# Hybrid attention / SSD / mixture-of-experts block: 1 / rms out of the SSD rows, one routing step less, combine and loads moved

## The chip, the cores and the metric

One core of a Trainium2 chip. The time is device microseconds of one execution of the whole program.

## The reference

One layer over 256 tokens of width 1024, in float32:

```
h = rmsnorm(x);  proj = h @ w_in      # q k v, indexer, z, xBC, dt, two gates
A: top-64 keys per query by an indexer under a block-causal mask, attention over them
B: conv, SiLU, chunked SSD scan, + D * x,
   yf = y * silu(z);  y_ssd = yf * rsqrt(mean(yf^2 per group of 512) + eps) * g   # 4 groups
merged = sigmoid(g_a) * (y_attn @ w_a) + sigmoid(g_b) * (y_ssd @ w_ssd)
x = x + merged @ w_out
h2 = rmsnorm(x);  top-1 of 4 expert groups, top-2 of its 8 experts, SwiGLU (hidden 256)
x = x + sum over the chosen experts of weight * down(silu(gate) * up)
```

The 2048 columns of y_ssd are four groups; each row (token) has one rsqrt per group.

## The kernel before, in words

All products up to W_out are made in three passes of split operands: each float is a high part plus a low part, and `PASSES` (L233) multiplies high-high, high-low, low-high. Weights of the projections come as chunks (class `Chunk`, L130): `raw` tiles are loaded on SP's queue (tag R, 4 buffers), ScalarE copies the high part (L152), VectorE or GpSimd (POOL) subtracts the low part (L156), into split tiles (tag S, 6 buffers). `next_w` (L219) also starts the load and the split of the chunk after the one that it hands out, so on SP's queue the weights of a chunk stand one chunk ahead of its products. A scheduler orders each engine's instructions by priorities and a timeline of its own; `tc.issue_after(i)` holds the block behind instruction i on i's engine.

The stages: attention with its projections; the SSD branch; the branch products; W_out with the residual and the router's logits; routing; the experts.

*SSD branch.* For each group g, four projection chunks (`xs_chunk`, `z_chunk`) are interleaved with `steps`: x (transposes), e (decays), y and T. `ssd_y` (L738) makes 512 columns in a tile yg: py products of 64 rows, L755 and L756 on VectorE, then the square (L758, ScalarE) into the z tile, whose tag has two buffers, and the sum over columns (L760 to L763, POOL). `ssd_tail` (L765) sums over partitions (ps_n), takes the power -0.5 on POOL, spreads r over all partitions by two products with the identity (ps_r, L775), multiplies yg by gain and r (L781, VectorE), and splits it into yT (L783 on ScalarE, L784 on VectorE).

*Branch products* (L826 to L847). yT holds 16 blocks of 128 columns. Loops: half of the SSD columns i (outside), half of the output columns c, halves of the tokens t. `wide_chunk` (L283) accumulates 8 blocks in one PSUM bank per t, token half 1 lagging by 3 blocks. L832 multiplies by the gate (tanh + 1); for i = 0 POOL adds it to the attention part (L834), for i = 1 VectorE does (L836), TensorE transposes and the result is split into mT.

*Loads of expert weights.* There are 8 quarters of 4 experts, 12 tiles each (8 gate/up, 4 down) of 1 MB, 96 in all, loaded by `prefetch` (L255) on SP's queue behind the last raw load traced so far. `PF0`, `PF1` and `PFO` (L1189 to L1199) say at which step how many tiles go into which buffers: tag E into space of their own, X into the space that the SSD pools leave (`xp`, L823), L into yT's buffers, then H, A, R, S, G. After the first 25 tiles all buffers are given out, and each later tile takes the buffer of a used one (`ring`, L1013).

*Routing and experts.* `route` (L935) finds for each token half the group (L942 to L946), the two experts and the slots; Dm is the 0/1 matrix of tokens by slots. `gather` (L1026) makes the normalised rows of the slots, x1 times Dm, VectorE moves them to xg (L1033); `gate_up` (L1035) multiplies. In quarter 0 `GA` (L1172) gives the order of gathers and gate/ups, and `combine` (L985: 11 VectorE and 3 ScalarE instructions and a transpose) is held behind `routed`, the last Dm. One float32 product shows as two records on TensorE.

Of the kernel before, what the change touches and what calls it, by code (L numbers as in the profile page):

```python
# [11 lines left out]
F32 = mybir.dt.float32  # L12
# [4 lines left out]
ALU = mybir.AluOpType  # L17
# [31 lines left out]
def block_kernel(ctx, tc, xin, idn, ngain, catt, cprep, cssd, cmoe, cwr, wsm, wwide, win, wgu, wdn, out, dbg=None):  # L49
# [633 lines left out]
    snorm = C("snorm")  # L683
    yT = [bigt([P, 2, 4, T], F32R, f"yT{g}") for g in range(4)]
# [53 lines left out]
    def ssd_y(g, q):  # L738
# [3 lines left out]
        st_[g, q, "yg"] = yg  # L742
# [3 lines left out]
        for h2 in range(2):  # L746
# [9 lines left out]
            dve.tensor_tensor(yg[:, h2, :], yg[:, h2, :], zs[:, h2, :], op=ALU.mult)  # L756
        sq = zs_t[g, q]
# [7 lines left out]
    def ssd_tail(g):  # L765
# [4 lines left out]
        r = ssd.tile([P, 2], F32, tag="nv", name="nv")  # L770
        dve.tensor_scalar(r, ps_n, 1.0 / 512, 4 * EPS, op0=ALU.mult, op1=ALU.add)
        power(r, r, None)
        ps_r = paux.tile([P, T], F32, tag="n", bufs=1, name="ps_r")
        for t in range(2):
            pe.matmul(ps_r[:, t * P:(t + 1) * P], lhsT=r[:, t:t + 1].to_broadcast([P, P]), rhs=ident,  # L775
                      start=True, stop=True)
        for q in range(2):
            yg = st_[g, q, "yg"]
            for b in range(2):
                ct = 4 * g + 2 * q + b  # L780
                dve.scalar_tensor_tensor(yg[:, b, :], yg[:, b, :], snorm[:, ct:ct + 1], ps_r, op0=ALU.mult, op1=ALU.mult)  # L781
            hl = yT[g][:, :, 2 * q:2 * q + 2]
            act.copy(hl[:, 0], yg)  # L783
            dve.tensor_sub(hl[:, 1], yg, hl[:, 0].bitcast(F32))  # L784
# [41 lines left out]
    for i in range(2):  # L826
        for c in range(2):
            ps = wide_chunk("S", yT[2 * i:2 * i + 2], LAG)
            for t in range(2):
                ta, tb = tab[t, c][:, 0], tab[t, c][:, 1]  # L830
                m = mo2.tile([P, 512], F32, tag="y", name="mg")
                dve.scalar_tensor_tensor(m, tb, 1.0, ps[t], op0=ALU.add, op1=ALU.mult)  # L832
                if i == 0:
                    pool.tensor_add(ta, m, ta)  # L834
                    continue
                dve.tensor_add(m, m, ta)  # L836
# [9 lines left out]
            if i:  # L846
                prefetch(PF1[2 * c] + PF1[2 * c + 1])  # L847

# [86 lines left out]
    def route(t):  # L935
# [9 lines left out]
        dve.tensor_scalar(gv[:, t, :], gv[:, t, :], gf[:, t:t + 1], -1e30, op0=ALU.is_lt, op1=ALU.mult)  # L945
# [68 lines left out]
    for q in range(8):  # L1014
# [26 lines left out]
        if q:  # L1041
            for k in (0, 4):
                gather(k, 4)
        else:
            for k in GA:
                gather(k[0], k[1])
                for kk in range(*k[2:]):
                    gate_up(kk)
# [262 lines left out]
```

## Time and profile before

| | us |
|---|---|
| median of 3 runs | 583.99 |
| the runs | 583.7, 583.99, 587.01 |
| the profiled execution, its own time | 585.1 |
| its span, first to last instruction | 583.3 |
| TensorE busy in it | 552.6 (95%) |
| VectorE / ScalarE / POOL busy | 330.9 / 271.8 / 239.5 |
| mean granted clock of TensorE | 0.987 |

The page gives one execution: busy time per engine, the span in slices, DMA queues, the chain of work that ended last, and the costliest groups of instructions. Times inside it count from the span's start. A busy TensorE is not TensorE at its peak, since matmuls overlap and their ends are modelled.

### The profile page before, as it was taken

The page shows a single profiled execution, that of the slowest core. Times are in us where ns is not written, and L with a number is a line of the kernel's source. Part 1 is how long each engine was busy: PE and PEld are TensorE (multiplying, and loading weights), DVE is VectorE, ACT ScalarE, POOL GpSimd, SP SyncE. Part 2 cuts the span into 40 slices and gives each one's busy share as a digit, 9 for nine tenths or more (in the row PEclk, how much of TensorE's full clock was granted, in tenths as well). Part 3 has the DMA queues.
Part 4 walks back from the last instruction along what each step waited for, and adds up shares of the span by engine and source line. Part 5 has one row for each costly group of instructions (what it writes and reads, how often), then busy time and mean ns, then how long its engine had stood idle before and what let it go on. Part 6 is the DMA issues. An engine that isn't in the chain of part 4 may idle for free.

```text
span 583.3 us, 9898 instructions
## 1 busy us (share of the span) xinstructions
PE 552.6 (95%) x3605; PEld 400.6 (69%) x3605; DVE 330.9 (57%) x689; ACT 271.8 (47%) x633; POOL 239.5 (41%) x254
## 2 busy tenths in 40 slices
PE   8999989999999999999999999999998898988976
PEld 5878768798898999898878888964453452433512
DVE  3659975999996778989695657451111121111101
ACT  7567557757987877878764436410000000000001
POOL 4687584775844456656567745210000000000000
PEclk9999999999999999999999999999989997999989
DMA  7755244453435488645568589989999999999993
GB/s 272 250 162 169 103 147 146 144 174 124 128 122 186 149 323 334 217 149 185 208 194 300 177 307 389 405 344 417 419 417 408 420 417 421 409 415 421 420 407 123
DMA packets 35123, 159.27 MB, mean 273 GB/s; under 512 B 4096, under 2 KB 5760, under 8 KB 25856
## 3 DMA queue, kind: packets, MB, share of 16 engines
q1 hardware_dynamic: 33776, 157.30, 71.8%
q10 hardware_dynamic: 1296, 1.30, 0.7%
q8 instruction: 30, 0.49, 0.3%
q14 instruction: 21, 0.17, 0.1%
HBM read 157.54 MB, written 1.05 MB: 272 GB/s over the span
## 4 chain that ended last, share of the span: by engine, by line
PE 69%; DMA 12%; DVE 9%; issue 4%; POOL 3%; ACT 3%; SPq 0%; ACTq 0%; POOLq 0%; DVEq 0%
PE ps_S L294 8%; PE pgu L1037 6%; PE ps_xs L241 6%; PE ps_g L294 6%; DMA we<-wdn 5%; DMA we<-wgu 5%; PE ps_z L241 5%; PE py L1097 4%; PE ps_A L294 4%; PE acc L1112 4%; PE ps_g L1030 4%; PE ps_q L294 3%; PE ps_o L241 2%; PE ps_o L294 2%; PE ps_iq L294 2%
## 5 line engine op out<-in xcount | busy, mean ns | idle before, releaser
L156 POOL TENSOR_TENSOR w_hl<-w_raw,w_hl 128x512 fp32r<-128x512 f32 (+1 forms) x101 | 141.6, 1406 | 81.8 <-ACT w_hl L152 66.5
L152 ACT CAST w_hl<-w_raw 128x512 fp32r<-128x512 f32 (+1 forms) x212 | 125.7, 620 | 46.4 <-PE ps_S L294 18.5
L156 DVE TENSOR_TENSOR w_hl<-w_raw,w_hl 128x512 fp32r<-128x512 f32 (+1 forms) x111 | 100.4, 911 | 38.7 <-ACT w_hl L152 38.1
L1055 POOL TENSOR_TENSOR dc<-Dm,cmr 128x128 f32<-128x128 f32 x16 | 6.1, 401 | 143.5 <-DVE Dm L960 137.4
L1037 PE MATMUL pgu<-we,xg 128*32 128x512 f32 x512 | 60.2, 603 | 3.9 <-DMA we<-wgu 3.9
L241 PE MATMUL ps_z<-hT,w_hl 128*128 128x256 f32 x384 | 51.7, 286 | 0.0
L241 PE MATMUL ps_xs<-hT,w_hl 128*128 128x256 f32 x384 | 50.7, 285 | 0.0
L241 PEld LDWEIGHTS ps_z<-hT,w_hl 128*128 128x128 f32 x384 | 47.8, 190 | 2.0 <-issue 2.0
L241 PEld LDWEIGHTS ps_xs<-hT,w_hl 128*128 128x128 f32 x384 | 47.6, 191 | 2.1 <-issue 2.1
L294 PE MATMUL ps_g<-w_hl,gT 128*128 128x512 f32 x192 | 48.1, 399 | 0.0
L294 PE MATMUL ps_S<-w_hl,yT 128*128 128x512 f32 x192 | 44.6, 391 | 0.0
L1033 DVE TENSOR_TENSOR xg<-ps_g,cmoe 128x512 f32<-128x512 f32 (+2 forms) x18 | 11.3, 631 | 57.4 <-PE ps_g L1030 57.4
L1030 PEld LDWEIGHTS ps_g<-Dm,x_sb 128*128 128x128 f32 x256 | 31.0, 191 | 14.9 <-issue 9.7
L294 PEld LDWEIGHTS ps_g<-w_hl,gT 128*128 128x128 f32 x192 | 34.9, 188 | 9.3 <-DVE w_hl L156 1.0
L294 PEld LDWEIGHTS ps_S<-w_hl,yT 128*128 128x128 f32 x192 | 35.8, 188 | 7.4
L1037 PEld LDWEIGHTS pgu<-we,xg 128*32 128x32 f32 x512 | 15.1, 110 | 37.1 <-issue 26.1
L1097 PE MATMUL py<-we,aTt 128*32 128x512 f32 (+1 forms) x272 | 35.8, 616 | 3.8 <-DVE aTt L1083 2.1
L1108 ACT COPY y<-py 128x512 f32<-128x512 f32 (+1 forms) x9 | 4.8, 539 | 66.9 <-PE py L1097 66.9
L1075 DVE SCALAR_TENSOR_TENSOR ac<-th,pgu 128x256 f32<-128x256 f32 x8 | 3.4, 421 | 57.5 <-ACT th L1073 57.5
L1112 PE MATMUL acc<-y,dcT 128*128 128x512 f32 (+1 forms) x68 | 32.6, 606 | 0.9 <-DVE y L1110 0.8
L1030 PE MATMUL ps_g<-Dm,x_sb 128*128 128x128 f32 x256 | 33.4, 280 | 0.0
L1073 ACT ACTIVATE th<-pgu,rs 128x256 f32<-128x256 f32 x8 | 3.8, 474 | 55.1 <-PE pgu L1037 55.1
(296 smaller groups left out, 968.9 us busy)
## 6 DMA issues: line engine op xcount, KB each, us to landing
we<-wgu SPq DMA_DIRECT2D x55, 1024.0 KB, 13.8
w_raw<-wwide SPq DMA_DIRECT2D x60, 512.0 KB, 3.9
w_raw<-win SPq DMA_DIRECT2D x44, 512.0 KB, 3.9
we<-wdn SPq DMA_DIRECT2D x17, 1024.0 KB, 17.4
we<-wdn SPq DMA_DIRECT2D x28, 512.0 KB, 12.0
we<-wgu SPq DMA_DIRECT2D x18, 512.0 KB, 10.2
x_sb<-xin SPq DMA_DIRECT2D x2, 512.0 KB, 4.4
we<-wdn SPq DMA_DIRECT2D x4, 256.0 KB, 11.5
```

What stands on the lines that cost most here:

```text
L152: return act.copy(self.hl[i][:, 0], self.raw[i])
L156: return eng.tensor_sub(hl[:, 1], self.raw[i], hl[:, 0].bitcast(F32))
L241: pe.matmul(ps, lhsT=lhs[k][:, a], rhs=rhs[k][:, b], start=j == 0 and k == 0 and i == 0, stop=j == len(regions) - 1 and k == KD - 1 and i ...
L294: pe.matmul(ps[t], lhsT=lhs[t][k][:, a], rhs=w[k][:, b], start=k == 0 and i == 0, stop=k == KD - 1 and i == 2)
L1030: pe.matmul(ps[:, kk, :], lhsT=x1[:, t, (k + kk) * P:(k + kk + 1) * P], rhs=Dm[:, t].rearrange("p e j -> p (e j)"), start=t == 0, stop=t == 1)
L1033: dve.tensor_tensor(xg[:, ks, :], ps, fgain[:, ks].unsqueeze(2).to_broadcast([P, n, P]), op=ALU.mult)
L1037: i = pe.matmul(pgu[32 * e:32 * e + 32, :], lhsT=xg[:, k, 32 * e:32 * e + 32], rhs=wg[k][e], start=k == 0, stop=k == KD - 1, tile_position ...
L1055: pool.tensor_tensor(dc[:, t], Dm[:, t], cmr[:, t, 4 * q:4 * q + 4].unsqueeze(2).to_broadcast([P, 4, NSLOT]), op=ALU.mult)
L1073: act.activation(th, pgu[:, 0:256], AF.Tanh, scale=rs)
L1097: i_py = pe.matmul(py[32 * e:32 * e + 32, :], lhsT=aTt[:, f, 32 * e:32 * e + 32], rhs=wd[2 * n + f][e][:, c], start=f == 0, stop=f == 1, t ...
L1108: act.copy(y, py)
L1112: pe.matmul(acc[t][n][:, c], lhsT=dcT[:, t * P:(t + 1) * P], rhs=y, start=False, stop=q == 7 and c.stop == 512)
```

## The change

`ssd_y` splits yg times gain into yT at once; `ssd_tail` keeps only r, in a small tile rg. The branch products run with the column half c outside and accumulate each group of 4 blocks in a bank of its own; what comes out of PSUM is multiplied there by r of its group. The tiles of gate b get "+ 1" once. The host's order of the weights follows. One X tile is loaded behind each of the first three chunks, two L tiles behind the fourth and two behind W_out's first. In `route`, the table `gio` is scaled by 1e30 and one instruction takes the place of two. In quarter 0 the gathers of k = 0 and 1 and the first gate/up come first, `combine` is held behind the second eviction, and the gathers of k = 2, 3 and 4 to 7 behind the gate/up before them.

```diff
@@ ssd_y
+        hl = yT[g][:, :, 2 * q:2 * q + 2]
+        for b in range(2):
+            ct = 4 * g + 2 * q + b
+            act.activation(hl[:, 0, b], yg[:, b], AF.Copy, scale=snorm[:, ct:ct + 1])
+            dve.scalar_tensor_tensor(hl[:, 1, b], yg[:, b], snorm[:, ct:ct + 1], hl[:, 0, b].bitcast(F32),
+                                     op0=ALU.mult, op1=ALU.subtract)
         sq = zs_t[g, q]
@@ ssd_tail
-        r = ssd.tile([P, 2], F32, tag="nv", name="nv")
+        r = rg[:, g]
         dve.tensor_scalar(r, ps_n, 1.0 / 512, 4 * EPS, op0=ALU.mult, op1=ALU.add)
         power(r, r, None)
-        ps_r = paux.tile([P, T], F32, tag="n", bufs=1, name="ps_r")
-        for t in range(2):
-            pe.matmul(ps_r[:, t * P:(t + 1) * P], lhsT=r[:, t:t + 1].to_broadcast([P, P]), rhs=ident,
-                      start=True, stop=True)
-        for q in range(2):
-            yg = st_[g, q, "yg"]
-            for b in range(2):
-                ct = 4 * g + 2 * q + b
-                dve.scalar_tensor_tensor(yg[:, b, :], yg[:, b, :], snorm[:, ct:ct + 1], ps_r, op0=ALU.mult, op1=ALU.mult)
-            hl = yT[g][:, :, 2 * q:2 * q + 2]
-            act.copy(hl[:, 0], yg)
-            dve.tensor_sub(hl[:, 1], yg, hl[:, 0].bitcast(F32))
@@ branch products
-    for i in range(2):
-        for c in range(2):
-            ps = wide_chunk("S", yT[2 * i:2 * i + 2], LAG)
-            for t in range(2):
+    for c in range(2):
+        for t in range(2):
+            act.activation(tab[t, c][:, 1], tab[t, c][:, 1], AF.Copy, bias=1.0)
+        U = [mo2.tile([P, 512], F32, tag="y", name="mg") for _ in range(2)]
+        for i in range(2):
+            w = pairs(next_w(), slice(0, 512))
+            src = pairs(yT[2 * i:2 * i + 2], slice(0, T))
+            pss = {}
+            for k in range(KD + LAG):
+                for t in range(2):
+                    kk = k - LAG * t
+                    if not 0 <= kk < KD:
+                        continue
+                    g = kk // 4
+                    if kk % 4 == 0:
+                        pss[t, g] = (pacc.tile([P, 512], F32, tag=f"acc{t}1", name="ps_S") if g
+                                     else pmm.tile([P, 512], F32, tag="mm", name="ps_S"))
+                    for a, b in PASSES:
+                        pe.matmul(pss[t, g], lhsT=src[kk][:, a, t * P:(t + 1) * P], rhs=w[kk][:, b],
+                                  start=kk % 4 == 0 and (a, b) == PASSES[0], stop=kk % 4 == 3 and (a, b) == PASSES[2])
+            for g, t in ((0, 0), (0, 1), (1, 0), (1, 1)):
                 ta, tb = tab[t, c][:, 0], tab[t, c][:, 1]
-                m = mo2.tile([P, 512], F32, tag="y", name="mg")
-                dve.scalar_tensor_tensor(m, tb, 1.0, ps[t], op0=ALU.add, op1=ALU.mult)
-                if i == 0:
-                    pool.tensor_add(ta, m, ta)
+                ps, m, r1 = pss[t, g], U[t], rg[:, 2 * i + g, t:t + 1]
+                if 2 * i + g == 0:
+                    act.activation(m, ps, AF.Copy, scale=r1)
+                elif 2 * i + g < 3:
+                    dve.scalar_tensor_tensor(m, ps, r1, m, op0=ALU.mult, op1=ALU.add)
+                    if i:
+                        dve.tensor_mul(m, m, tb)
+                        pool.tensor_add(ta, m, ta)
+                if 2 * i + g < 3:
                     continue
+                dve.scalar_tensor_tensor(m, ps, r1, tb, op0=ALU.mult, op1=ALU.mult)
                 dve.tensor_add(m, m, ta)
...
-            if i:
-                prefetch(PF1[2 * c] + PF1[2 * c + 1])
+            prefetch(PF1[2 * c + i])
@@ route
-        dve.tensor_scalar(gv[:, t, :], gv[:, t, :], gf[:, t:t + 1], -1e30, op0=ALU.is_lt, op1=ALU.mult)
-        dve.tensor_tensor(em[:, t].rearrange("p (g e) -> p g e", g=4), E[:, t].rearrange("p (g e) -> p g e", g=4),
-                          gv[:, t].unsqueeze(2).to_broadcast([P, 4, 8]), op=ALU.add)
+        dve.scalar_tensor_tensor(em[:, t].rearrange("p (g e) -> p g e", g=4),
+                                 gv[:, t].unsqueeze(2).to_broadcast([P, 4, 8]), gf[:, t:t + 1],
+                                 E[:, t].rearrange("p (g e) -> p g e", g=4), op0=ALU.subtract, op1=ALU.add)
@@ experts, quarter 0
-            for k in GA:
-                gather(k[0], k[1])
-                for kk in range(*k[2:]):
-                    gate_up(kk)
+            gathered = [gather(0, 1), gather(1, 1)]
+            i_gu = gate_up(0)
+            for k, n, a, b in GA:
+                with tc.issue_after(i_gu.ins):
+                    gather(k, n)
+                for kk in range(a, b):
+                    i_gu = gate_up(kk)
         if q == 0:
-            with tc.issue_after(routed.ins):
+            with tc.issue_after(gathered[1].ins):
                 combine()
@@ tables
-GA = ((0, 1, 0, 0), (1, 1, 0, 1), (2, 2, 1, 2), (4, 4, 2, 4))
+GA = ((2, 2, 1, 2), (4, 4, 2, 4))
-PF1 = ("X", "X", "X", "L")
-PFO = ("L", "L", "L", "")
+PF1 = ("X", "X", "X", "LL")
+PFO = ("LL", "", "", "")
```

## Rows read from the trace of the kernel before

**Rows 1.** The page's line of memory traffic, 40 slices of 14.6 us.
```profile
GB/s 272 250 162 169 103 147 146 144 174 124 128 122 186 149 323 334 217 149 185 208 194 300 177 307 389 405 344 417 419 417 408 420 417 421 409 415 421 420 407 123
```

**Rows 2.** The chain that ended last, 480 to 583: start us, us, what.
```profile
541.82 19.88 DMA we<-wgu
...
561.74 1.94 PE pgu L1037 x8
```

**Rows 3.** Stretches: engines' busy us (count), granted clock, DMA share, GB/s.
```profile
340.00:388.00 48.00, 47.74 (x298) 40.74 (x297) 27.69 (x77) 20.52 (x52) 16.11 (x15) 1.00 1.00 390
388.00:391.00 3.00, 3.00 (x27) 1.87 (x30) 0.75 (x3) 0.00 (x0) 0.76 (x2) 1.00 0.51 128
391.00:392.00 1.00, 1.00 (x9) 0.21 (x2) 0.00 (x0) 0.00 (x0) 0.00 (x0) 1.00 0.69 287
392.00:561.70 169.70, 151.56 (x1067) 67.17 (x1066) 28.07 (x66) 10.40 (x22) 5.31 (x14) 0.97 1.01 417
```

**Rows 4.** SP's queue, timeline 380 to 390: start us, us, what.
```profile
380.67 0.42 SPq L270 DMA_DIRECT2D we<-wgu  x1
...
389.39 0.33 SPq L270 DMA_DIRECT2D we<-wgu  x1
```

**Rows 5.** The same table by stretches: branch products, late SSD stage.
```profile
307.40:352.80 45.40, 45.40 (x208) 37.76 (x209) 26.60 (x39) 20.50 (x36) 28.04 (x24) 1.00 0.78 262
216.00:280.00 64.00, 63.84 (x523) 58.47 (x522) 60.73 (x105) 50.28 (x113) 40.73 (x35) 1.00 0.65 229
```

**Rows 6.** The chain that ended last, 186 to 320: a tail's broadcast products.
```profile
292.88 0.64 PE ps_r L775 x4
```

**Rows 7.** Timeline of TensorE, 261 to 262: another tail's broadcast products.
```profile
261.59 0.61 PE L775 MATMUL ps_r<-ident,nv 128*128 128x128 f32 x4
...
262.04 0.27 PE L716 MATMUL ps_x<-ident,xs 128*128 128x128 f32 x1
```

**Rows 8.** VectorE by form, 200 to 360: busy us, mean ns, idle before.
```profile
L784 DVE TENSOR_TENSOR yT<-yg,yT 128x512 fp32r<-128x512 f32 x8 | 7.8, 974 | 0.3 <-ACT yT L783 0.3
...
L606 DVE SCALAR_TENSOR_TENSOR xs<-xs,acc 128x256 f32<-128x256 f32 x10 | 7.0, 716 | 0.0
...
L781 DVE SCALAR_TENSOR_TENSOR yg<-yg,cssd,ps_r 128x256 f32<-128x256 f32 x16 | 6.6, 473 | 0.1
...
L832 DVE SCALAR_TENSOR_TENSOR mg<-tab,ps_S 128x512 f32<-128x512 f32 x8 | 5.3, 678 | 1.7 <-PE ps_S L294 1.7
```

**Rows 9.** ScalarE by form, 200 to 360.
```profile
L783 ACT CAST yT<-yg 128x512 fp32r<-128x512 f32 x8 | 5.1, 637 | 0.9 <-DVE yg L781 0.9
...
L701 ACT ACTIVATE zs<-ps_z 128x256 f32<-128x256 f32 x12 | 4.7, 390 | 7.2 <-DVE zs L702 4.7 <-POOL ysum L761 1.7 <-POOL ysum L763 0.6
```

**Rows 10.** ScalarE by form, 0 to 140.
```profile
L501 ACT ACTIVATE tab<-ps_g,rh 128x512 f32<-128x512 f32 x8 | 5.4, 686 | 0.5 <-PE ps_g L294 0.5
...
L184 ACT ACTIVATE gT<-ps_h,gcol 128x256 fp32r<-128x256 f32 x8 | 3.1, 484 | 0.0
```

**Rows 11.** Timelines 381 to 404: routing steps, first gather, first gate/up.
```profile
383.62 0.35 DVE L945 TENSOR_SCALAR gv<-gv,gf 128x4 f32<-128x4 f32 x2
383.88 0.32 DVE L946 TENSOR_TENSOR em<-logit,gv 128x32 f32<-128x32 f32 x2
384.11 0.31 DVE L948 MAX8 rm<-em 128x8 f32<-128x32 f32 x2
...
386.38 1.95 PE L1030 MATMUL ps_g<-Dm,x_sb 128*128 128x128 f32 x16
...
387.25 0.29 DVE L1033 TENSOR_TENSOR xg<-ps_g,cmoe 128x128 f32<-128x128 f32 x1
...
388.26 1.07 PE L1037 MATMUL pgu<-we,xg 128*32 128x512 f32 x8
```

**Rows 12.** SP's queue, timeline 316 to 338: weights and the first X loads.
```profile
316.28 2.15 SPq L141 DMA_DIRECT2D w_raw<-wwide  x2
...
337.84 1.24 SPq L270 DMA_DIRECT2D we<-wdn  x1
```

More of the change, by code (lines that the diff above doesn't have):

```diff
@@ L683, in block_kernel @@
     snorm = C("snorm")
+    rg = cst.tile([P, 4, 2], F32, name="rg")
     yT = [bigt([P, 2, 4, T], F32R, f"yT{g}") for g in range(4)]
@@ L741, in ssd_y @@
         yg = ssd.tile([P, 2, T], F32, tag="yg", name=f"yg{g}{q}", bufs=YB)
-        st_[g, q, "yg"] = yg
         if q == 0:
@@ L1032, in gather @@
             ks = slice(k, k + n)
-            dve.tensor_tensor(xg[:, ks, :], ps, fgain[:, ks].unsqueeze(2).to_broadcast([P, n, P]), op=ALU.mult)
+            return dve.tensor_tensor(xg[:, ks, :], ps, fgain[:, ks].unsqueeze(2).to_broadcast([P, n, P]), op=ALU.mult)
         def gate_up(k):
@@ L1252, in prep @@
     halves = [slice(0, 512), slice(512, 1024)]
-    wide += [wa[:, :, o] for o in halves] + [ws[:, 8 * i:8 * i + 8, o] for i in range(2) for o in halves]
+    wide += [wa[:, :, o] for o in halves] + [ws[:, 8 * i:8 * i + 8, o] for o in halves for i in range(2)]
     wwide = np.stack(wide + [wo[:, :, 0:512]])
@@ L1274, in prep @@
         "cos": c16, "sin": s16,
-        "gio": _bcast(np.arange(4, 0, -1).astype(f)),
+        "gio": _bcast(np.arange(4, 0, -1).astype(f) * f(1e30)),
         "sio": _bcast(np.where(np.arange(1, 33) <= CAP, np.arange(1, 33), -1).astype(f)),
```

## The prediction

> **What bounds the kernel now.** Three views, in this order. The first is the page's line of memory traffic over forty slices of 14.6 us: about 100 to 330 GB/s in the first half, then over 400 from slice 27 to the last but one [rows 1]. So the last 190 us could be a stage that waits for expert weights. The second, the chain that ended last, says so: it ends in long pieces of expert transfers, the last of them landing at 561.74 us, and only then comes TensorE's tail of 21.6 us to the end of the span [rows 2]. The third, a table by stretches, says when this stream begins and whether it ever stops [rows 3]: the DMA engines are full from 340 to 388 us (share 1.00), half idle from 388 to 391 (128 GB/s), and full again from 392 to 561.7 (417 GB/s). The stop is short and decides this case. 25 expert tiles of 1.05 MB fit in the buffers. The last half tile that needed no routed expert was issued at 380.67 us; the next issue on SP is at 389.39 [rows 4], right after the first four gate/up products of expert quarter 0 freed a buffer. From there 71 tiles follow at 1.05 MB / 417 GB/s = 2.51 us each, 178 us, whatever the compute engines do. So the end is the moment at which the first gate/up product is done, plus a fixed stream and a fixed tail. That moment lies at the end of a long stretch in which TensorE is the bound: 63.84 of 64 us busy in the late SSD stage and 45.40 of 45.40 us in the branch products [rows 5].
>
> Two consequences for pricing. TensorE work taken out before 386 us moves the end by its length. Earlier loads alone fill the same 25 buffers sooner and then wait longer, so they are worth little by themselves.
>
> **SSD rows without 1 / rms.** Each of the four tails loses two broadcast products (ps_r, four records each time). Where they cut into the py pairs the chain gives them 0.64 us [rows 6]; where they stand between other products the next one starts 0.45 us after them (261.59 to 262.04) [rows 7]. Two tails are of each kind: 2 x 0.64 + 2 x 0.45 = **2.2 us** of TensorE removed. The bounds are 4 x 0.45 = 1.8 and 4 x 0.64 = 2.6; I take 2.1, a little under the middle, because some of the 0.64 is the py pair's own restart.
>
> VectorE loses sixteen L781 (473 ns, one input in PSUM) and eight L784 (974 ns): 7.6 + 7.8 = 15.4 us. It gains sixteen 128x256 scalar_tensor_tensor whose two tensor inputs both lie in SBUF. The row with that shape is L606: 716 ns mean, against 473 for L781 [rows 8]. So 16 x 0.716 = 11.5 us, and VectorE is relieved by 3.9 us (bounds: relieved by 7.8 us if the new ones cost 473 ns, loaded with 0.2 more if they take the 974 ns of the 512-wide L784). ScalarE loses eight copies of 637 ns (L783 [rows 9]) and gains sixteen scaled copies of 128x256; the scaled copy of that shape into the same type is L184, 484 ns [rows 10]: 7.7 - 5.1 = 2.6 us more, beside TensorE. Both engines lie beside TensorE here (60.73 and 50.28 us busy of 64 [rows 5]), so I count neither; what it costs if that cover goes is the slower rival below, what it brings if VectorE was the hidden bound the faster one.
>
> In the branch products each of the four (token half, column half) pairs now needs four evacuations instead of two. VectorE gains, per pair, one scalar_tensor_tensor from PSUM (678 ns, L832) and one product of two SBUF tiles (974 ns by L784, the same operands) [rows 8]: 4 x 1.65 = 6.6 us. ScalarE gains a scaled copy out of PSUM (686 ns by L501 [rows 10]) and one "plus 1" of the same size: 4 x 1.37 = 5.5 us. VectorE has 45.4 - 26.6 = 18.8 us free there and ScalarE 24.9 [rows 5], so this is hidden, price 0; the price if a quarter of the 12.1 us came through is +3. The wait that is added is ScalarE's, on a half-done chunk; behind it in its queue stand weight casts, which TensorE needs. The early half of a chunk is read while the late half still accumulates in another bank, so no PSUM buffer is held longer than before. The order of chunks (column half outside) makes the first half of mT early and leaves the last chain, two VectorE operations and four transposes, as it was: 0.
>
> **One routing step less.** In each of two interleaved chains a tensor_scalar goes (383.62 to 383.88, 0.26 us for the pair), and a tensor_tensor becomes a scalar_tensor_tensor (its pair takes 0.23 us, 383.88 to 384.11) [rows 11]. L945 is a whole step of the chain: -0.26, and I give back 0.03 for the longer instruction: **-0.23 us** (bounds 0 and -0.3).
>
> **Combine behind the first gather.** TensorE's sixteen gather records start at 386.38, so the first four, k = 0, are out by 386.38 + 4 x 0.122 = 386.87; its eviction starts only at 387.25, between combine's VectorE instructions, and TensorE runs all sixteen before the first gate/up at 388.26 [rows 11]. After the change only eight records precede it: TensorE is free at 387.36, the eviction (0.29 us) can run from about 387.05, and the gate/up starts near 387.45: **-0.8 us** (bounds 0, if the eviction stays at 387.25 and the order holds, and -1.0, TensorE's eight records). Combine moves 11 VectorE and 3 ScalarE instructions some 1.2 us later. The evictions k = 2 to 7 queue behind it on VectorE, POOL's dc and TensorE's transposes of it behind them; between its first use and now lie the gate/ups of k = 0 to 3, 4 x 1.07 = 4.3 us, so 0.
>
> **Loads from the first chunk on.** SP takes its queue in order. The X loads move from 337.84 us, behind the fourth chunk's weights, to behind the second chunk's (316.28) and the third's [rows 12]. Two of the three are thus done before 340, 2 x 2.51 = 5.0 us less queue, and the 25 tiles are in at about 383.4 instead of 388.4; the last of them cannot come much earlier, because they wait for buffers that W_out's products free up to 380.67. The weights queued behind an X load come up to 2.5 us later. They have a lead of six split tiles, 6 x 1.41 = 8.5 us at 11.3 us (45.4 / 4) per chunk of eight. Price of the move: 0, both ways, except that it makes room for the rest: without it the 3.1 us below could not all be used.
>
> **Sum.** -2.1 - 0.23 - 0.8 = -3.1 us at the first gate/up: its load is issued at 386.3 instead of 389.4, after the buffers are full (383.4), so the stream moves by all of it. The profiled execution took 585.1 us with a span of 583.3; the sum gives 582.0 there. The median of the runs shown is 583.99, 1.1 below, and the forecast goes by it: **580.9 us**. A measurement of this kernel can tell about 1% from no change, 5.8 us; this is half of it.
>
> **Rivals.**
> *The early loads don't come early* (X1 stuck on SP behind SSD buffers still read). The buffers then fill at 388.4 as before, with the next load already waiting: no gap. The gap's worth is what 388 to 392 failed to move, (4 x 417 - 3 x 128 - 287) KB per us = 1.0 MB = 2.4 us: 581.6. Chance 0.1.
> *The loads bound everything*, and the two tiles come straight off the end: 5.0 us, 579.0. Against it the half idle stretch [rows 3]. Chance 0.06.
> *VectorE was the hidden bound of the SSD stage.* The page's chain runs there through VectorE for long pieces, and 60.73 of 64 us is nearly full. Then its 3.9 us come off too: 580.9 - 3.9 = 577.0. Against: TensorE's 63.84 of 64. Chance 0.16.
> *ScalarE late in the SSD stage* (slower). The square of a y step now stands behind two scaled copies, 2 x 0.484 = 0.97 us; POOL's ysum waits for the square, and with two zs buffers the tanh of a later z chunk waits for ysum. L701 already sits idle 7.2 us, of it 1.7 + 0.6 behind ysum [rows 9]. If six z chunks hand on 0.97 us each, 5.8 us, the time is 580.9 + 5.8 = 586.7. It decides once ysum becomes the last to arrive at most z chunks and the delay outlasts the queue of weights. Against: the same steps lose VectorE work. Chance 0.16. A rule stands beside this one: the Trainium skill, "GPSIMD Engine Reference", section 1, says that GpSimd shares its SBUF interfaces with VectorE and contends with VectorE instructions that have two SBUF inputs, as the sixteen new ones have. This trace agrees as far as L606 goes, mean 716 against 473 with a PSUM input; the page gives no price, and by it POOL's adds would be later still.
>
> **How the numbers follow.** The forecast itself has 0.52. Its own range, from the bounds of its terms (-1.8 to -4.0, and 0.5 of run spread), is 579.5 to 582.7. The two outer rivals lie at 577.0 and 586.7; the range 576.5 to 586.5 leaves out some tails of each. Faster by over 1% (under 578.2): most of the VectorE rival and a tail of the forecast, 0.15. Slower by over 1% (over 589.8): the far end of the ScalarE rival, 0.05. The rest is 0.80.
>
> **What would show it.** Right: no ps_r; the first gate/up near 385.2, the expert load behind it near 386.3 and the last landing near 558.6; a longer idle DMA stretch just before that load, ending at the same distance behind it; TensorE still full from 186 to 380. Wrong: TensorE with gaps in the branch products or SSD stage; a first gate/up that moves by much other than 3 us; a last landing that does not move with it.

## The result, and the profile after

The changed kernel takes **587.0 us**, the median of 19 runs (584.95 to 589.77), against 583.92 (582.17 to 587.01, 19 runs) for the kernel before. The ratio is **1.0051**, 95% interval 1.0040 to 1.0062. The forecast was 580.9 us with a range from 576.5 to 586.5: instead of 3.1 us faster it is 3.1 us slower and outside the range. It is half a per cent, within the 1% that the prediction had called no change, but with an interval clear of 1. The profiled execution took 586.69 us, its span is 584.9.

First the stretches of [rows 3] and [rows 5] again (length; busy us and instructions of PE, PEld, DVE, ACT, POOL; granted clock; DMA share; GB/s):

```profile
216.00:280.00 64.00, 63.40 (x513) 57.33 (x512) 62.98 (x101) 50.44 (x116) 40.32 (x36) 1.00 0.65 231
307.40:352.80 45.40, 44.51 (x203) 36.58 (x202) 32.77 (x45) 23.79 (x42) 30.73 (x23) 1.00 0.87 304
392.00:563.00 171.00, 153.54 (x1087) 69.30 (x1079) 28.09 (x67) 10.38 (x22) 5.34 (x15) 0.96 1.01 415
```

TensorE is no longer full: 0.6 us are missing in the late SSD stage, 0.9 in the branch products. VectorE, which was to be relieved of 3.9 us over the SSD stage, has 62.98 us of 64 where it had 60.73. In the branch products it has 32.77 against 26.60, which is near the 6.6 us counted there. What TensorE waited for is in the waits (line and tile, the instruction waited for, us in all, times, longest), the first from 205 to 280, the rest from 300 to 392:

```profile
PE ps_xs L241 <- DVE zs L703: 0.6, 1, 0.6
...
PE ps_o L241 <- ACT w_hl L152: 1.5, 1, 1.5
...
PE ps_lg L929 <- ACT xT L925: 0.9, 2, 0.5
PE ps_n L776 <- POOL ysum L768: 0.9, 1, 0.9
```

These are four places. One product waits for a zs tile near 223 us. The last sum of squares holds up its narrow product at 312 us: the product stands in order among the branch products, so these wait with it. The first narrow product of W_out (its last 512 columns come in two chunks of 256) waits at 359 us. And xT, the transposed rows that the router's product takes, stops TensorE twice at the end of W_out, where before it did once. The timeline of TensorE shows two of them, the wait in brackets:

```profile
313.13 0.61 PE L776 MATMUL ps_n<-ones,ysum 128*128 128x1 f32 x4 [0.90 <-POOL ysum L768]
...
360.74 0.38 PE L241 MATMUL ps_o<-w_hl,mT 128*128 128x256 f32 x1 [1.49 <-ACT w_hl L152]
```

The chain that ended last says why the second is late. The raw weights were issued at 349.82, right behind two of the early L loads (347.48 and 347.95 on SP), landed at 359.97, and ScalarE's cast had been waiting for them:

```profile
349.82 10.15 DMA w_raw<-win
360.03 0.04 issue
360.07 0.63 ACT w_hl L152
```

The next lines are the steps that answer to [rows 11], from timelines of VectorE and TensorE, and the end of the chain, which answers to [rows 2]:

```profile
385.63 0.41 DVE L964 SCALAR_TENSOR_TENSOR em<-gv,gf,logit 128x32 f32<-128x32 f32 x2
385.95 0.31 DVE L967 MAX8 rm<-em 128x8 f32<-128x32 f32 x2
...
388.27 1.05 PE L1049 MATMUL ps_g<-Dm,x_sb 128*128 128x128 f32 x8
389.49 1.07 PE L1056 MATMUL pgu<-we,xg 128*32 128x512 f32 x8 [0.16 <-DVE xg L1052]
```
```profile
545.01 19.85 DMA we<-wgu
564.90 1.11 PE pgu L1056 x8
```

The first gate/up comes at 389.49 instead of 388.26, the load behind it is issued at 390.62 instead of 389.39 [rows 4]. The last load lands at 564.86 (545.01 + 19.85), where 558.6 was forecast.

A table by stage says more than absolute times, because the profiled execution of before had begun its SSD products about 1 us later than every other one here (152.15 us; the others 150.4 to 151.6). All times are from the timelines of TensorE and VectorE (first xs product, first attention product, first W_out product, logit, first gate/up). The last two columns are two kernels of the experiments; they differ in the SSD rework alone.

| us | before | after | e13: order, loads, old tail order | e14: after, old tail order |
|---|---|---|---|---|
| SSD stage (xs to A) | 126.44 | 125.18 | 126.44 | 125.20 |
| attention and branch products (A to W_out) | 74.48 | 76.72 | 74.46 | 76.70 |
| W_out, router (to logit) | 29.51 | 31.82 | 29.04 | 30.29 |
| routing, gather (to gate/up) | 5.68 | 4.91 | 4.90 | 4.90 |
| sum | 236.11 | 238.63 | 234.84 | 237.09 |

The changed kernel gains 1.3 and 0.8 us in the first and last stage and loses 2.2 and 2.3 in the two between: 2.5 us later at the first gate/up, most of the 3.1 us in the medians.

### The profile page after: what moved, and what is told of

Its sections match the earlier page's. It is cut to its first block, busy times and chain, and to the rows that moved or that the text cites. A ratio compares the mean times of both kernels' runs of the same rounds, so it can differ in the third digit from the quotient of the medians.

```text
span 584.9 us, 9882 instructions
## 1 busy us (share of the span) xinstructions
PE 550.2 (94%) x3589; PEld 399.4 (68%) x3589; DVE 341.8 (58%) x687; ACT 277.2 (47%) x649; POOL 245.8 (42%) x254
## 3 DMA queue, kind: packets, MB, share of 16 engines
HBM read 157.54 MB, written 1.05 MB: 271 GB/s over the span
## 4 chain that ended last, share of the span: by engine, by line
PE 56%; DVE 19%; DMA 9%; ACT 6%; issue 5%; POOL 4%; ACTq 0%; SPq 0%; DVEq 0%; POOLq 0%
PE pgu L1056 8%; PE ps_S L840 6%; PE py L1120 5%; DVE w_hl L156 5%; PE ps_g L1049 5%; PE ps_xs L241 4%; PE acc L1135 4%; DMA we<-wdn 3%; DMA we<-wgu 3%; PE ps_z L241 3%; PE ps_o L241 2%; DVE acc L603 2%; PE ps_iq L294 2%; PE ps_A L294 2%; PE ps_k L294 2%
## 5 line engine op out<-in xcount | busy, mean ns | idle before, releaser
L156 POOL TENSOR_TENSOR w_hl<-w_raw,w_hl 128x512 fp32r<-128x512 f32 (+1 forms) x101 | 145.1, 1442 | 77.7 <-ACT w_hl L152 63.4
L156 DVE TENSOR_TENSOR w_hl<-w_raw,w_hl 128x512 fp32r<-128x512 f32 (+1 forms) x111 | 105.4, 958 | 24.2 <-ACT w_hl L152 23.5
L1056 PE MATMUL pgu<-we,xg 128*32 128x512 f32 x512 | 58.5, 595 | 4.9 <-DMA we<-wgu 4.7
L840 PE MATMUL ps_S<-w_hl,yT 128*128 128x512 f32 x192 | 45.1, 392 | 0.0
L1049 PEld LDWEIGHTS ps_g<-Dm,x_sb 128*128 128x128 f32 x256 | 32.5, 197 | 18.0 <-issue 13.6
L1120 PE MATMUL py<-we,aTt 128*32 128x512 f32 (+1 forms) x272 | 38.2, 647 | 4.5 <-DVE aTt L1106 2.6
L1049 PE MATMUL ps_g<-Dm,x_sb 128*128 128x128 f32 x256 | 35.1, 286 | 0.0
L1135 PE MATMUL acc<-y,dcT 128*128 128x512 f32 (+1 forms) x68 | 30.5, 574 | 0.1
```

The lines of the kernel that those rows point to most:

```text
L156: return eng.tensor_sub(hl[:, 1], self.raw[i], hl[:, 0].bitcast(F32))
L840: pe.matmul(pss[t, g], lhsT=src[kk][:, a, t * P:(t + 1) * P], rhs=w[kk][:, b], start=kk % 4 == 0 and (a, b) == PASSES[0], stop=kk % 4 == 3 ...
L1049: pe.matmul(ps[:, kk, :], lhsT=x1[:, t, (k + kk) * P:(k + kk + 1) * P], rhs=Dm[:, t].rearrange("p e j -> p (e j)"), start=t == 0, stop=t == 1)
L1056: i = pe.matmul(pgu[32 * e:32 * e + 32, :], lhsT=xg[:, k, 32 * e:32 * e + 32], rhs=wg[k][e], start=k == 0, stop=k == KD - 1, tile_position ...
L1120: i_py = pe.matmul(py[32 * e:32 * e + 32, :], lhsT=aTt[:, f, 32 * e:32 * e + 32], rhs=wd[2 * n + f][e][:, c], start=f == 0, stop=f == 1, t ...
L1135: pe.matmul(acc[t][n][:, c], lhsT=dcT[:, t * P:(t + 1) * P], rhs=y, start=False, stop=q == 7 and c.stop == 512)
```

## The experiments

Every ratio is to the kernel before on the same chip, with its 95% interval.

**The parts alone.**

`e1`, the changed kernel with the loads in their old places:
```diff
-PF1 = ("X", "X", "X", "LL")
-PFO = ("LL", "", "", "")
+PF1 = ("", "", "XX", "XL")
+PFO = ("L", "L", "L", "")
```


> The changed kernel with the loads of expert weights where they stood before (X, X behind the third branch chunk, X, L behind the fourth, three L along W_out); all else as changed. Theory A (the loads put in front make W_out's narrow weights late: TensorE stops 1.65 us there in the changed kernel, and ScalarE's copies of mT wait behind the cast that waits for them): the 1.65 us stop goes, the first gate/up comes 1.5 to 2 us earlier than 389.5, ratio to the kernel before about 1.002. Theory B (the rebuilt SSD and branch stage costs it, whatever the loads do): the stop stays within 0.5 us, ratio 1.004 to 1.006 as for the whole change.

`e2`, the kernel before with the early loads:
```diff
-            if i:
-                prefetch(PF1[2 * c] + PF1[2 * c + 1])
+            prefetch(PF1[2 * i + c])
...
-PF1 = ("X", "X", "X", "L")
-PFO = ("L", "L", "L", "")
+PF1 = ("X", "X", "X", "LL")
+PFO = ("LL", "", "", "")
```


> The kernel before with the early loads alone. Theory A: TensorE stops before W_out's narrow products as in the changed kernel, the first gate/up comes 1 to 2 us later than 388.3, ratio 1.002 to 1.004. Theory B: no new stop, the buffers fill earlier and wait longer, ratio 0.999 to 1.001.

`e3`, the kernel before with the routing step and the gather order (the hunks of the change at L945 and from L1030 on):
```diff
...
-            for k in GA:
-                gather(k[0], k[1])
...
+            gathered = [gather(0, 1), gather(1, 1)]
+            i_gu = gate_up(0)
...
```


> The kernel before with the routing step less and the new order of the first gathers, gate/ups and combine alone. Both theories: from the first logit step to the first gate/up 0.8 us less than the 5.7 us of before (382.58 to 388.26), the end earlier by about that, ratio 0.9985. A third theory (what moves is what the scheduler places differently anywhere in the program after any edit): TensorE's order changes far from the edit too, and the first logit step moves by more than 0.5 us either way.

`e4`, the changed kernel with those hunks and the loads undone, so that the SSD rework is left:
```diff
...
-            gathered = [gather(0, 1), gather(1, 1)]
...
+PF1 = ("", "", "XX", "XL")
+PFO = ("L", "L", "L", "")
```


> The changed kernel with old routing, old order of the first gathers and old places of the loads: the SSD and branch rework alone. Theory A: 2 us of TensorE gone, less about 1 us that TensorE waits for the last ysum: first gate/up about 1 us earlier than 388.3, ratio 0.998. Theory B: the waits added in the branch stage and in W_out take more than the 2 us: first gate/up 1 us or more later, ratio 1.002 to 1.005.

Measured: e1 1.0077 (1.0050 to 1.0105), e2 1.0029 (1.0006 to 1.0051), e3 **0.9982** (0.9968 to 0.9995), e4 **1.0108** (1.0078 to 1.0137). The order gains what was forecast for it; the SSD rework costs more than the whole change. That the moved loads make the loss falls with e1: without them it is no smaller (the intervals overlap). But e2 is odd, since nothing stops TensorE there before 377 us. Its stretches at the routing stage and its timeline:

```profile
382.00:386.00 4.00, 4.00 (x11) 1.58 (x12) 2.75 (x22) 0.00 (x0) 0.00 (x0) 0.50 1.03 408
```
```profile
378.64 1.16 PE L910 MATMUL ps_lg<-cwr,xT 128*128 128x36 f32 x8 [0.35 <-ACT xT L906]
379.63 0.41 PE L900 MATMUL ps_hf<-ident,x_sb 128*128 128x128 f32 x2
380.50 1.93 PE L910 MATMUL ps_lg<-cwr,xT 128*128 128x36 f32 x8 [0.46 <-ACT xT L906]
382.23 4.89 PE L866 MATMUL ps_w<-on 128*128 128x512 bf16 x11
...
388.49 1.95 PE L1029 MATMUL ps_g<-Dm,x_sb 128*128 128x128 f32 x16
```

The granted clock of the stretch is 0.50: TensorE runs at 1.2 instead of 2.4 GHz, behind two stops for xT; the four us on either side have 0.82 and 0.83. The eleven fillers (ps_w: products of ones whose result nobody reads, put there to keep TensorE busy) stand in order ahead of the rank product and take 4.89 us instead of the 2.54 of e3. VectorE had its first selection by 384.6 and waits for the rank product behind them. e1 and e4 show 0.67 and 0.50 in the stretch from 386 to 390, so part of their loss is the clock. The trace of the changed kernel has 1.00 there.

**Attempts at the stops and the clock.**

`e5`, the changed kernel with the late loads behind W_out's narrow weights:
```diff
-PF1 = ("X", "X", "X", "LL")
-PFO = ("LL", "", "", "")
+PF1 = ("X", "X", "X", "")
+PFO = ("LL", "LL", "", "")
```


> The changed kernel with its four late half-tile loads (L) issued two and two behind the raw loads of W_out's two narrow chunks instead of ahead of them; the six early ones (X) stay. Waits theory: the narrow raw lands about as early as in the kernel before, the 1.65 us stop of TensorE ahead of the first narrow product of W_out goes, W_out ends 1 to 1.7 us sooner, the first gate/up product comes at 388 instead of 389.5 us, and the ratio falls from 1.005 to about 1.002. Clock theory: the stop goes but the routing stage meets the 1.2 GHz level in some executions all the same, so the median stays at 1.004 to 1.006 and the profile may show 0.5 in the granted clock between 380 and 392 us.

(The L loads are whole tiles of 1.05 MB, not half tiles.)

`e6`, the changed kernel, sums ahead of the split of yT:
```diff
-        hl = yT[g][:, :, 2 * q:2 * q + 2]
...
         sq = zs_t[g, q]
         act.activation(sq, yg, AF.Square)
...
+        hl = yT[g][:, :, 2 * q:2 * q + 2]
...
```


> The changed kernel with the squares and GpSimd's sums of the SSD stage issued ahead of the split of yT. Waits theory: the sum of the last group is ready sooner, the 1.06 us stop of TensorE at 311.9 us goes, and all that follows is about 1 us sooner (ratio 1.003 to 1.004). Rival: ScalarE's square now delays the split instead and the branch product stops for yT, so nothing is gained (ratio 1.005 or more).

`e7` is e2 with fewer fillers, `e8` the same with the order of e3:
```diff
-WARM = (9, 3, 10, 11, 3, 3)
+WARM = (9, 3, 10, 4, 3, 3)
```


> The kernel before with the early loads alone, as in the run of that part, but with 4 instead of 11 filler matmuls behind the router product. Clock theory: where the granted clock is 0.5 in the routing stage, the 11 fillers took 4.89 us ahead of the rank product and 4 take at most 1.8 us, so the rank product waits for its selection instead, the first gather comes 2 to 2.5 us sooner after the router product than in the run with 11 (4.0 us instead of 6.4 from the logit), and the ratio falls from 1.003 to about 0.998. Rival (the fillers were not what the first gather waited for, or fewer of them let the gather itself run at 1.2 GHz): the ratio stays at 1.002 to 1.004.

> The kernel before with the routing step, the order of the first gathers and the early loads of the change, without its SSD rework, and with 4 filler matmuls. Sum of the parts by the clock theory: the order alone gave 0.998, and early loads without the late fillers give back nothing or another 1 us: ratio 0.995 to 0.998, faster than both kernels. Rival: early loads cost by themselves (ScalarE's and GpSimd's queues, shared with the raw weights): ratio 1.000 to 1.003.

Measured: e5 1.0097 (1.0079 to 1.0116) and e6 1.0097 (1.0071 to 1.0124), both slower than the changed kernel. In e5 the weights are early enough and TensorE stops at the same place, for another engine:

```profile
361.21 0.98 PE L241 MATMUL ps_o<-w_hl,mT 128*128 128x256 f32 x6 [1.76 <-DVE w_hl L156]
```

VectorE is busy without a gap from 348.37 to 361.4 there, with evacuations ahead of the split of those weights: the last of them runs from 356.01 to 357.79, two splits from 357.71 to 361.15. In e6 the wait for the sum is 0.2 us shorter and the branch products stop for a weight split instead:

```profile
312.44 0.61 PE L777 MATMUL ps_n<-ones,ysum 128*128 128x1 f32 x4 [0.71 <-POOL ysum L762]
312.91 0.48 PE L841 MATMUL ps_S<-w_hl,yT 128*128 128x512 f32 x1
314.68 1.67 PE L841 MATMUL ps_S<-w_hl,yT 128*128 128x512 f32 x6 [1.29 <-DVE w_hl L156]
```

So the stop moves from one engine's queue to another's: from the first xs product to the first gate/up e5 takes 238.42 us, the changed kernel 238.63. That lies in VectorE, ScalarE and POOL together. Why e5 is slower than the changed kernel all the same is not shown: its profiled execution (587.25) is the shortest of its four. In e6 (240.11) the clock falls as well, to 0.74 from 386 to 390. e7 is 1.0039 (1.0020 to 1.0059), e8 1.0006 (0.9991 to 1.0021): fewer fillers don't cure the low clock. Logit to first gather is 5.1 us in e7, between the 6.4 of e2 and the 3.8 of the kernel before, as six more fillers and the rank products still run at 1.2 GHz.

`e9` (order, loads) and `e11` (the changed kernel) put fillers where xT stops TensorE:
```diff
-                    pe.transpose(phf[:, kk, t - ts[0], :], x1[:, t, k * P:(k + 1) * P], ident)
+                    i_hf = pe.transpose(phf[:, kk, t - ts[0], :], x1[:, t, k * P:(k + 1) * P], ident)
+            if c > 1:
+                warm2(2, i_hf)
```


> The kernel before with the routing step, the gather order and the early loads of the change, the 11 fillers behind the router product as before, and two more fillers (128x512 of ones, into a spare PSUM tile) behind each of the last three pairs of transposes of W_out, so that TensorE has work while xT is copied. Clock theory: what precedes the fall of the granted clock to 1.2 GHz in the routing stage are the two stops of 0.5 and 0.6 us for xT; with work in them the clock stays at 2.4 GHz until the experts, first gather at about 385 us, and the ratio is 0.994 to 0.998. Rival: the clock falls all the same (0.5 in the profile between 380 and 388 us), ratio 1.000 to 1.003.

> The changed kernel with the same six fillers behind the last three pairs of transposes of W_out. Clock theory: in some executions of the changed kernel the clock falls in the routing stage as in four of its relatives; with fillers it doesn't, and the median falls from 587.0 by 1 to 1.5 us (ratio 1.002 to 1.004); the stops at 312 and 359 us stay. Rival (the median of the changed kernel is its stops alone): ratio 1.004 to 1.007.

Measured 1.0118 (1.0096 to 1.0140) and 1.0112 (1.0084 to 1.0141). They failed as tests of the fillers: the extra PSUM tile changed the rotation of the buffers, W_out's last products went behind the transposes one row half after the other, and in e9 the logit came 3.3 us later than in e3. But e11 says something on the stops themselves: two for xT (0.45 and 1.00 us) and two more of 0.52, and a granted clock of 1.00 from 140 to 408 us.

`e10`, the kernel before with the branch products in column order, 1/rms still in yT:
```diff
-    for i in range(2):
-        for c in range(2):
+    for c in range(2):
+        for i in range(2):
...
-    wide += [wa[:, :, o] for o in halves] + [ws[:, 8 * i:8 * i + 8, o] for i in range(2) for o in halves]
+    wide += [wa[:, :, o] for o in halves] + [ws[:, 8 * i:8 * i + 8, o] for o in halves for i in range(2)]
...
```


> The kernel before with the branch products of the SSD in the order of the change (columns outside, row halves inside), 1/rms still in yT, loads in their old places by chunk. If the order makes the stops of the SSD rework (it needs the yT of groups 2 and 3 one chunk, 11.4 us, sooner): TensorE stops for yT or for ps_n near 312 us by 1 us or more, and of the 1.0108 of the SSD part at least half, ratio 1.005 or more. If the added evacuations make them (eight products by r on VectorE and ScalarE): no stop at 358 to 360 us, ratio 0.999 to 1.003.

Measured 1.0054 (1.0034 to 1.0075). It has no stop near 312 us, but one of 0.43 that ends at 360.09, the two xT stops, and the low clock again (granted 0.63 from 382 to 386). The ratio is the one expected if the order of columns costs; the place is not, for it is W_out and its tail.

**The tail put back by hand.** In before and in e3, with one xT stop, the last eight W_out products stand behind the transposes of the third column chunk, so that VectorE and ScalarE make xT beside them; in e2, with two stops, all stand ahead. This edit holds the last nine back:
```diff
...
+                        if ts[0] and k >= KD - HOLD:
+                            late.enter_context(tc.issue_after(hf2.ins))
...
+            if c == 2:
+                hf2 = i_hf
...
+HOLD = 3
```
`e12` is e2 with it, `e13` order and loads with it, `e14` the changed kernel with it.

> The kernel before with the early loads alone, as in the run of that part (ratio 1.0029), but with the last nine W_out products of the second row half held back until the transposes of the third column chunk are issued, so that the tail of W_out has the kernel before's order: one stop for xT in place of two. Clock theory: what precedes the fall to 1.2 GHz in the routing stage are the two stops; with one the granted clock stays 1.0 until the experts, the 11 fillers take 2.54 us again, the first gather comes at 385 to 386 us instead of 388.5, and the ratio is 0.997 to 1.000. Rival (the clock falls there for another reason, or the early loads cost by themselves): 0.5 in the profile between 378 and 392 us all the same, or a ratio of 1.002 or more.

> The kernel before with the routing step, the gather order and the early loads of the change and the held back products; no SSD rework. Clock theory: the gain of the order (0.9982) is kept and that of the early loads (about 1 us sooner at the router) is added: no 0.5 before 400 us, ratio 0.995 to 0.998, faster than both kernels. Rival: ratio 1.000 or more, as with the loads and the order without the hold (1.0006).

> The changed kernel with the same products held back: one xT stop instead of two (0.9 us less), and by the clock theory no fall of the clock in the routing stage in any execution. Then what is left of the loss is the stops at 222, 312 and 359 us (0.8, 1.06, 1.65 us) against the 2.1 us saved by ps_r and the 0.8 us of the order: the ratio falls from 1.005 to 0.999 to 1.002. Rival (the stops ahead of W_out make the loss, the tail does nothing): 1.004 to 1.006.

Measured: e12 1.0004 (0.9991 to 1.0017), e13 **0.9970** (0.9954 to 0.9986; 582.37 us, 12 runs), e14 1.0058 (1.0035 to 1.0080). e12, its stretch and its timeline, against e2 above:

```profile
382.00:386.00 4.00, 4.00 (x26) 2.39 (x25) 3.69 (x31) 0.48 (x3) 0.00 (x0) 1.00 1.03 412
```
```profile
380.20 1.14 PE L919 MATMUL ps_lg<-cwr,xT 128*128 128x36 f32 x8 [0.24 <-ACT xT L915]
381.17 2.54 PE L866 MATMUL ps_w<-on 128*128 128x512 bf16 x11
...
385.04 1.95 PE L1038 MATMUL ps_g<-Dm,x_sb 128*128 128x128 f32 x16
```

One stop, the clock stays at 1.00, the fillers take 2.54 us, the first gather comes 3.5 us sooner (385.04 against 388.49). The median of e13 is below those of both kernels, with intervals that don't touch. e14 shows the other side: with the tail mended and the clock at 1.00 in its profile the changed kernel stays where it was. Its waits keep two of the stops:

```profile
PEld ps_n L776 <- POOL ysum L768: 1.3, 1, 1.3
PEld ps_o L241 <- ACT w_hl L152: 1.1, 1, 1.1
```

**The two halves of the SSD rework**, each on the tail of e13. `e15` is e13 with the loops of e10. `e16` is e14 with the old loop order:
```diff
-    for c in range(2):
...
-        for i in range(2):
+    for i in range(2):
+        for c in range(2):
...
-                if 2 * i + g == 0:
+                if g == 0:
                     act.activation(m, ps, AF.Copy, scale=r1)
...
+                dve.scalar_tensor_tensor(m, ps, r1, m, op0=ALU.mult, op1=ALU.add)
+                dve.scalar_tensor_tensor(m, tb, 1.0, m, op0=ALU.add, op1=ALU.mult)
...
```


> The kernel of the order, the early loads and the held back products (0.9970), with the branch products of the SSD in column order as in the change; 1/rms stays in yT. If the order of columns costs by itself: TensorE stops for yT near 312 us or ahead of W_out by 1 us or more, ratio 1.001 or more. If its cost alone (1.0054) was the tail's order and the clock: no stop over 0.6 us between 300 and 385 us, no 0.5 before 400 us, ratio 0.996 to 0.999.

> The changed kernel with the held back products and the branch products in the old order (row halves outside); 1/rms still goes into their evacuation (per chunk and row half one scaled copy on ScalarE, two products on VectorE, and the sum). If the evacuations and the yT split are what costs: stops at 222 us and ahead of W_out as in the changed kernel, first gate/up at 387.5 us or later, ratio 1.003 to 1.006. If the column order is: those stops go, the 2.1 us of ps_r stay, ratio 0.993 to 0.997.

Measured: e15 1.0064 (1.0041 to 1.0088), e16 1.0043 (1.0027 to 1.0059), against 0.9970 without either. Each half costs by itself, and they don't add. e16 keeps the stops at 223 us (zs, 0.6) and 313:

```profile
313.70 0.61 PE L776 MATMUL ps_n<-ones,ysum 128*128 128x1 f32 x4 [0.88 <-POOL ysum L768]
```

In e15 TensorE is full until W_out (45.40 us of the 45.40 from 307.4 to 352.8), then come two stops, and behind them the low clock, this time in W_out itself (timeline; the stretch from 360 to 364 has a granted clock of 0.57):

```profile
359.30 0.39 PE L241 MATMUL ps_o<-w_hl,mT 128*128 128x256 f32 x1 [1.28 <-ACT w_hl L152]
360.02 1.90 PE L241 MATMUL ps_o<-w_hl,mT 128*128 128x256 f32 x8 [0.34 <-DVE w_hl L156]
```

ScalarE's cast of the narrow weights waits 2.1 us there for their transfer, which was issued at 349.28, right behind two early loads (348.23 and 348.70), and landed at 358.53. In e13 the same cast waits 1.0 us and TensorE doesn't stop.

## Why the prediction was wrong, by its own steps

**What bounds the kernel: right in kind.** In e3, e12 and e13 a sooner first gate/up gives a sooner end. In the changed kernel the load behind it moves by the same 1.23 us as the gate/up itself. But "a fixed stream and a fixed tail" is not so fixed: from the first gate/up to the end of the span it is 195.0 us before and 195.4 after, and 193.7 (e12) to 197.5 (e15) over all eighteen profiles. And "whatever the compute engines do" left something out: the last half tiles were issued until 382.03, so the buffers were not full at 383.4 (the DMA engines have a share of 1.04 from 386 to 390), and the third load came 2.1 us later (395.68 against 393.56), since the whole gather of four tiles now stands ahead of the third gate/up.

**ps_r: right.** The spacing of its records in the trace of before is 1.09 us for the first two tails together and 1.00 for the last two, 2.1 us as taken, and it is gone in all kernels with the rework.

**Routing step and gather order: right.** em to MAX8 takes 0.32 us where the two steps took 0.49, so 0.17 of the 0.23; gather to gate/up 1.22 us where it was 1.88, so 0.66 of the 0.8. e3 alone gains 0.18%.

**Moved loads, price 0: right only with the tail held.** e13 against e3 is 0.3 us in the sum by stage, within what can't be told apart. But with the loads moved the order in which W_out's tail was issued became another one, and that cost some 0.25% (e2 against e12, whose intervals overlap; those of e8 and e13 don't, but they differ in the fillers too).

**The step that failed** is the pricing of the SSD rework on the other engines: "Both engines lie beside TensorE here", "so I count neither", and for the branch products "so this is hidden, price 0". It named a price for the case that this fails (+3 us) but gave that no chance. e14 against e13 gives it: 237.09 against 234.84 us at the first gate/up, **+2.25 where -2.1 was counted**. So the rework cost TensorE 2.25 + 2.1 = 4.3 us that were not counted. Stops are 2.9 of them, by the spacing of its records in e14: 0.8 near 223, 1.06 at 312, 1.0 at 359. The other 1.4 us stand in no wait: over these stages TensorE is busy 234.28 us in e13 and 234.27 in e14, though the records of ps_r are gone, so other products must follow one another less closely (those of ps_S take 45.1 us in e14, 44.6 in e13). What makes that was not found. For the stops there are two reasons.

First, the sum of free VectorE time was the wrong test. What counts is the place in the queue. VectorE, ScalarE and POOL each also make weight tiles for TensorE, and an evacuation that stands ahead of a split delays the split however empty the engine is on average. That is seen in e5 and e6, where curing one stop opened the next one on another engine. The text named this queue ("behind it in its queue stand weight casts, which TensorE needs") and priced it at 0.

Second, VectorE was not relieved. Its forms from 200 to 360 (busy us, mean ns, idle before), after, and from 200 to 320 in e13, whose SSD stage is that of before:

```profile
L756 DVE TENSOR_TENSOR yg<-yg,zs 128x256 f32<-128x256 f32 x16 | 12.1, 756 | 0.2
L762 DVE SCALAR_TENSOR_TENSOR yT<-yg,cssd,yT 128x256 fp32r<-128x256 f32 x16 | 11.9, 746 | 2.2 <-ACT yT L761 2.2
L606 DVE SCALAR_TENSOR_TENSOR xs<-xs,acc 128x256 f32<-128x256 f32 x10 | 8.7, 883 | 0.1
L755 DVE SCALAR_TENSOR_TENSOR yg<-xs,hsk,py 128x256 f32<-128x256 f32 x16 | 7.5, 470 | 0.0
```
```profile
L756 DVE TENSOR_TENSOR yg<-yg,zs 128x256 f32<-128x256 f32 x16 | 10.1, 631 | 0.2
...
L606 DVE SCALAR_TENSOR_TENSOR xs<-xs,acc 128x256 f32<-128x256 f32 x10 | 7.0, 716 | 0.0
```

The new instructions take 746 ns, near the 716 taken for them. But two groups that the change doesn't touch grew, 631 to 756 and 716 to 883, together 16 x 0.125 + 10 x 0.167 = 3.7 us, and that is the relief. They have two SBUF inputs; L755, with one in PSUM, stays at 470.

The single records of the changed kernel show where the time goes. Five of the sixteen L762 ran with no POOL instruction beside them and took 484 to 486 ns, not 716. Ten began while a POOL instruction ran; nine of these took 701 to 1459 ns, and each ended 0.28 us after that POOL instruction (the tenth began just before POOL's end and took 473). L756 does the same: 408 to 426 ns alone (eight), up to 1507 with POOL running (eight, each ending 0.28 us after POOL). L755 takes 468 to 481 either way. So 716 was the mean of two kinds, and the price of the new instructions hangs on what POOL runs at that moment. This agrees with the rule cited from the Trainium skill, "GPSIMD Engine Reference", section 1, on the interfaces that GpSimd shares with VectorE. The prediction drew from that rule only that POOL's adds would be later; here VectorE is held too. The stop near 223 us comes about that way (timeline of all engines):

```profile
220.43 1.73 POOL L156 TENSOR_TENSOR w_hl<-w_raw,w_hl 128x512 fp32r<-128x512 f32 x1
220.94 1.50 DVE L756 TENSOR_TENSOR yg<-yg,zs 128x256 f32<-128x256 f32 x1
...
222.48 0.51 ACT L761 ACTIVATE yT<-yg,cssd 128x256 fp32r<-128x256 f32 x1 [2.42 <-DVE yg L756]
...
222.90 0.36 ACT L702 ACTIVATE zs<-ps_z 128x256 f32<-128x256 f32 x1
...
223.43 0.41 DVE L703 SCALAR_TENSOR_TENSOR zs<-zs,ps_z 128x256 f32<-128x256 f32 x1
...
223.89 0.38 PE L241 MATMUL ps_xs<-hT,w_hl 128*128 128x256 f32 x1 [0.56 <-DVE zs L703]
```

POOL's weight split holds VectorE's L756, the new scaled copy on ScalarE (L761) waits 2.42 us for that, the z step (L702) stands behind the copy in ScalarE's queue, and TensorE waits for its second half (L703). In e5 the two splits that end at 361.15 took 3.44 us, while POOL made splits of its own; the one at 347.76 took 0.69. One group with two SBUF inputs, e<-e,cb, went the other way (956 to 830), so the change shuffled what lies beside what. No run takes POOL's work away, so how much of the 2.25 us this makes is open.

**The rivals.** "ScalarE late in the SSD stage" (586.7) came nearest in time, by luck, and named two of the waits, that of the zs tile and that for POOL's ysum. But they are 0.8 and 1.06 us, not 5.8, and another 1.0 lies in W_out, where no rival looked. VectorE as the hidden bound had the right engine and the wrong sign. The two rivals on the loads forecast a gain, which e2 and e12 don't show.

**Open.** The stages account for 2.25 us between e13 and e14; the medians differ by 4.6, the two spans by 3.4. In the profiles the first gate/up is 1.9 us apart and the end 3.4, so 1.5 us arise behind it, in the expert stream, and the profiled execution of e14 is the shortest of its six. What the others lose was not found. Nor is it known whether the changed kernel meets the low clock in executions that were not profiled; e14 says that mending its tail gains nothing that can be measured.

## What to carry to other kernels

An engine with idle time on average is not free: before pricing an added instruction at nothing, find what stands behind it in that engine's queue and whether the engine on the path waits for that, and compare all edits with the time by stage. Before taking a mean as a price, look whether it is the mean of two kinds, here 407 to 1517 ns in one group of ten (L606 before). After any edit look first at whether the scheduler kept the order of the last instructions ahead of a critical hand-over; here holding nine products in their old place seems worth more (0.25%) than the loads that had displaced them (no gain that can be told). Undo a combined change part by part: three edits here hold a gain of 0.3% and a loss that is larger.

## What the runs showed of the hardware that was not expected

The granted clock of TensorE falls to 1.2 GHz in the middle of busy stretches, and where it falls goes with stops that are short. In e1, e2, e4, e6, e8 and e10 the stretch with the low clock lies behind the second xT stop at the end of W_out (0.35 to 0.46 us each); in e7 behind these and within a third of 1.52 us; in e9 and e15 behind two stops earlier in W_out. In before, e3, e5, e12, e13, e14 and e16, with one xT stop, the clock is 1.00 from the SSD stage to the first experts. But the changed kernel has two xT stops and kept 1.00 in its one profile, e11 has two and kept it too, and e1 and e4 kept it through two stops near 360 us (1.08 and 0.84, 1.14 and 0.84). So such stops go before the fall without forcing it, and what decides is open.

Fillers that are to keep TensorE busy turn against the kernel when the clock falls: the same eleven took 2.54 us at 2.4 GHz and 4.89 at 1.2, in order ahead of the product that the routing waits for.

A VectorE instruction with two SBUF inputs that began while POOL ran one of its own ended 0.28 us after POOL in nearly every case (L756 and L762 in the changed kernel: 17 of 18), while the same instruction alone took 408 to 426 and 484 to 486 ns.
